# A routed-expert stage: experts of up to 64 tokens in whole fp32 products, and their place in the order

## The chip, the core and the metric

The kernel runs on one core of one Trainium2 chip. The metric is the device time of one execution in microseconds. Three runs of the kernel before took 2928.57, 2928.95 and 2931.59 us, median 2928.95.

## The reference

The program is a two-layer mixing block (gated scans, differential attention) followed by a second block, on 1024 tokens of 1024 features, in fp32. The change lies in the second block's routed experts. Each token picks 2 of 32 experts, and each expert computes

```
y = (silu(x @ w1[e]) * (x @ w3[e])) @ w2[e]      # w1, w3: 1024 x 512, w2: 512 x 1024
```

on its tokens' rows; the rows are weighted by their gates and added to the residual stream. The weights of one expert are 6 MB of fp32, those of all 192 MB.

## The kernel before, in words

Up to about 2075 us the kernel computes the first block, the convolution and recurrence of the second, and the routing. Then come 32 experts, one after the other, and after about 2805 us a final stage (a gated projection and a norm) that needs every expert's rows.

**Ranks and rooms.** The routing sorts the experts by their token count. Rank 0 is always expert 0, so that its weights can be loaded early; the others follow by falling count. `ROOM` (line 29) gives the rows that each rank gets: 256 for ranks 0 to 5, 128 for 6 to 12, 96 for 13 to 19 and 64 for 20 to 31. A 256 is handled as two blocks of 128 rows. `ORDER` (line 41) is the order in which the ranks are run: six groups, each of one 256 and then a slice of the ranks 6 to 31 in rising order. So the ranks of 64 stand in the last three groups: 3, 19, 20, 21, 22; 4, 23 to 26; 5, 27 to 31.

**Steps of an expert.** `expert_gather` fetches its token rows with an indirect DMA on POOL. `tokens` transposes them on TensorE (`rows_T`, line 1818) and splits them into a high part (ACT copy, rounded to fp32r) and a low part (DVE subtraction). `up`, `gate` and `down` are the three products. `down` scatters the rows with an indirect DMA on POOL to `ydd`. Line 1940's loop issues them so: gate of expert j, then gather, tokens and up of expert j+1, then down of expert j.

**Weights.** Each product has two tiles of 1 MB (`load`, line 1854), loaded on SP's in-order DMA queue into a ring of ten buffers (`raw`); a load waits until the tile ten places before it has been read. For a product in fp32r a tile is split into high and low parts (`split`, line 1637: ACT copy at line 1642, DVE subtraction at line 1643) into four split buffers (`ews`). After its split a raw tile is free.

**Products.** Blocks of more than 64 rows take `mm3` (line 371): three fp32r matmuls for each of the k slices (8 in up and gate, 4 for each half of the output in down). An expert of 64 takes another way in `mm`: high and low parts of the tokens stand side by side as the 128 columns of one stationary operand, and two matmuls (lines 1832 and 1833) multiply it by the weights' high and low parts. The product of the high part comes out in rows 0 to 63, that of the low part in rows 64 to 127, and `both` (line 1837) adds the halves on ACT and DVE. Its `down` doesn't split the weights: line 1912 multiplies the same 128 columns by the raw fp32 tile, which stays in the ring until TensorE has read it.

The order of instructions on each engine comes from the program's order as a scheduler rearranges it by its own estimate of when operands are ready.

Of the kernel before, what the change touches and what calls it, by code (L numbers as in the profile page):

```python
# [11 lines left out]
F32 = mybir.dt.float32  # L12
F32R = mybir.dt.float32r
# [3 lines left out]
AF = mybir.ActivationFunctionType  # L17
# [9 lines left out]
NE = 32  # L27

ROOM = [256] * 6 + [128] * 7 + [96] * 7 + [64] * 12
DBL = ROOM.count(256)  # L30
# [7 lines left out]
FAR = 36.0  # L38
NB = 2 * S // 128 + NE

ORDER = [q for d in range(DBL) for q in [d] + list(range(DBL + (NE - DBL) * d // DBL, DBL + (NE - DBL) * (d + 1) // DBL))]


def _chunks():
# [176 lines left out]
def r32(ap):  # L221
    return ap.bitcast(F32)
# [7 lines left out]
def kernel(ctx: ExitStack, tc: tile.TileContext, A: dict, out: bass.AP, upto=99, dbg=None):  # L230
    nc = tc.nc
    V, G, SC, T, SY = nc.vector, nc.gpsimd, nc.scalar, nc.tensor, nc.sync
# [138 lines left out]
    def mm3(ps, ah, al, bh, bl, first, last):  # L371
        T.matmul(ps, ah, bh, start=first, stop=False)  # L372
        T.matmul(ps, ah, bl, start=False, stop=False)  # L373
        T.matmul(ps, al, bh, start=False, stop=last)  # L374

    def feat(ps_pool, w, c0, m, half):

        wh, wl = w
        p = ps_pool.tile([128, 512], F32, tag="acc", name="pF")
        t = slice(half * 512, half * 512 + 512)  # L380
        for k in range(8):
            mm3(p[:m], wh[:, k, c0:c0 + m], wl[:, k, c0:c0 + m], ATh0[:, k, t], ATl0[:, k, t], k == 0, k == 7)
        return p

    def tokm(ps_pool, w, n, i, c0=0, at=None, tag="acc"):

        wh, wl = w
        th, tl = at or (ATh0, ATl0)
        p = ps_pool.tile([128, 512], F32, tag=tag, name="pK")
        t = slice(i * 128, i * 128 + 128)  # L390
        for k in range(8):
            mm3(p[:, :n], th[:, k, t], tl[:, k, t], wh[:, k, c0:c0 + n], wl[:, k, c0:c0 + n], k == 0, k == 7)
        return p
# [328 lines left out]
    for l in range(DEPTH):  # L722
# [104 lines left out]
        for i in range(8):  # L827
            p = tokm(pa, wi, 256, i)
# [18 lines left out]
        for half in range(2):  # L847
            t = slice(half * 512, half * 512 + 512)
            p = feat(pa, wg, 0, 32, half)
# [3 lines left out]
        for i in range(8):  # L853
            p = tokm(pa, wv, 256, i)
            SC.activation(gvv[:, i, :], p[:, :256], AF.Copy)
        with tc.high_priority(AHEAD):
            for tt in range(2):
# [4 lines left out]
                for j in range(2):  # L862
                    t = slice(j * 512, j * 512 + 512)
                    p = pm.tile([128, 512], F32, tag="mm", name="pu")
# [12 lines left out]
                    a, pU = scan_intra(sw, pm, o, False, gvv, tt * 128, j)  # L877
# [351 lines left out]
    def half(j):  # L1229
        return slice(j * 512, j * 512 + 512)  # L1230
# [25 lines left out]
    def conv_tile(f):  # L1256
        w = load_w(wp, A["w2in"][f], 8, 256, G)
        if f in PE_CONV:
            return conv_blocks(f, w)
        u = shifted("u")  # L1260
        for j in range(2):
            us = u[:, 32 + j * 512:544 + j * 512]
            SC.activation(us, feat(pa, w, 0, 128, j), AF.Copy)
            sg = bt.tile([128, 512], F32, tag="sg", name="sgc", bufs=2)
            SC.activation(sg, feat(pa, w, 128, 128, j), AF.Sigmoid)
            G.tensor_tensor(us, us, sg, op=OP.mult)

        for t in (half(0), half(1)) if f == 0 else (slice(0, S),):
            y, at = Y[f][:, t], lambda k: u[:, 2 + k + t.start:2 + k + t.stop]
            SC.activation(y, at(0), AF.Identity, scale=cw[:, f, 0:1], bias=VC("cb")[:, f:f + 1])  # L1270
            for k in range(1, 31):
                V.scalar_tensor_tensor(y, at(k), cw[:, f, k:k + 1], y, op0=OP.mult, op1=OP.add)
# [136 lines left out]
    with act_set("sigmoid_and_others", True):  # L1409
        blocks = [conv_tile(f) for f in range(4)]  # L1410
# [208 lines left out]
    ew = ews.enter_context(tc.tile_pool(name="ew", bufs=2))  # L1619
    rings.append(xw.enter_context(tc.tile_pool(name="raw2", bufs=6, side="right")))  # L1620
    ewx = xw.enter_context(tc.tile_pool(name="ewx", bufs=3, side="right"))
    first = []
# [14 lines left out]
    def split(s_, eng):  # L1637

        j = wturn[0] % 4
        wturn[0] += 1  # L1640
        w = whs[j >= 2].tile([128, 2, 4, 512], F32R, tag="w", name="ews")
        SC.activation(w[:, 0], s_, AF.Copy)  # L1642
        eng.tensor_tensor(w[:, 1], s_, r32(w[:, 0]), op=OP.subtract)  # L1643
        return w[:, 0], w[:, 1]

    with tc.tile_pool(name="rw", bufs=1) as rw, tc.tile_pool(name="rp", bufs=1, space=PSUM) as rp, \
# [129 lines left out]
        for c in range(2):  # L1776
            wh = ew.tile([128, 2, 512], F32R, tag="xh", name="wpleh", bufs=3)
            wl = ew.tile([128, 2, 512], F32R, tag="xl", name="wplel", bufs=3)
# [4 lines left out]
        for i in range(0, 8, 2):  # L1783
            eo = [ew.tile([128, D], F32, tag="ys", name="eo") for _ in range(2)]
            for c in range(2):
                for n in range(2):
                    p = pp.tile([128, 512], F32, tag="acc", name="pe")
# [30 lines left out]
    def rows_T(src, n, th, tl, m):  # L1818

        for g in range(0, m, 4):  # L1820
            p = ept.tile([128, 4, 128], F32, tag="mm", name="pT")
            for j in range(4):
                T.transpose(p[:, j, :n], src[:n, (g + j) * 128:(g + j + 1) * 128], ident[:n, :n])  # L1823
            last = (SC.activation(th[:, g:g + 4, :n], p[:, :, :n], AF.Copy),
                    V.tensor_sub(tl[:, g:g + 4, :n], p[:, :, :n], r32(th[:, g:g + 4, :n])))
        return last

    def mm(n, p, ah, al, k, bh, bl, first, last):


        if n <= 64:
            T.matmul(p, ah[:, k, :], bh, start=first, stop=False)
            T.matmul(p, ah[:, k, :], bl, start=False, stop=last)
        else:
            mm3(p[:n], ah[:, k, :n], al[:, k, :n], bh, bl, first, last)

    def both(dst, p, n):
        SC.activation(dst, p[64:64 + n], AF.Copy)
# [8 lines left out]
    class Expert:  # L1847
# [2 lines left out]

        def __init__(self, e, blocks):
            self.e, self.blocks = e, blocks

        def load(self, name):
            src = A[name][ds(self.e, 1)].rearrange("o c p k f -> c p (o k f)")
            r = []
            for c in range(2):
                s_ = raw()
                SY.dma_start(s_.rearrange("p a b -> p (a b)"), src[c])
                r.append(s_)  # L1860
            return r

        def tokens(self):
            self.X = []
            for xb, n, dst in self.blocks:
                xh = ew.tile([128, 8, 128], F32R, tag="xh", name="xh", bufs=3)
                xl = xh[:, :, 64:] if n <= 64 else ew.tile([128, 8, 128], F32R, tag="xl", name="xl", bufs=3)
                self.last = rows_T(xb, n, xh, xl, 8)
                self.X.append((xh, xl))

        def product(self, raws):
            ps = [eph.tile([128, 512], F32, tag="h", name="h") for _ in self.blocks]
            for c in range(2):
                wh, wl = raws[c] if isinstance(raws[c], tuple) else split(raws[c], V)
                for (xb, n, dst), (xh, xl), p in zip(self.blocks, self.X, ps):
                    for k in range(4):
                        mm(n, p, xh, xl, c * 4 + k, wh[:, k], wl[:, k], (c, k) == (0, 0), (c, k) == (1, 3))
            return ps

        def up(self, raws):  # L1880
# [15 lines left out]
        def down(self, raws):  # L1896
            Y2 = []
            for (xb, n, dst), hs in zip(self.blocks, self.hs):
                hh = ew.tile([128, 4, 128], F32R, tag="hh", name="hh")
                hl = hh[:, :, 64:] if n <= 64 else ew.tile([128, 4, 128], F32R, tag="hl", name="hl")  # L1900
                rows_T(hs, n, hh, hl, 4)
                Y2.append((hh, hl, ew.tile([128, D], F32, tag="ys", name="ys")))
            for c in range(2):
                whole = self.blocks[0][1] <= 64
                if not whole:
                    wh, wl = split(raws[c], V)
                for (xb, n, dst), (hh, hl, ys) in zip(self.blocks, Y2):
                    p = epy.tile([128, 512], F32, tag="y", name="py")
                    for k in range(4):
                        if whole:  # L1910

                            T.matmul(p, r32(hh[:, k, :]), raws[c][:, k], start=k == 0, stop=k == 3)
                        else:
                            mm(n, p, hh, hl, k, wh[:, k], wl[:, k], k == 0, k == 3)
                    if n <= 64:
                        both(ys[:n, half(c)], p, n)
                    else:
                        SC.activation(ys[:n, half(c)], p[:n], AF.Copy)
                    if c:
                        G.indirect_dma_start(out=ydd, out_offset=bass.IndirectOffsetOnAxis(ap=dst, axis=0),  # L1920
                                             in_=ys[:n], in_offset=None)
# [14 lines left out]

    x = ranked(ORDER[0])
    with tc.issue_after(x.last[0].ins), tc.issue_after(x.last[1].ins):
        w3 = [split(s_, V) for s_ in first[2:4]]
    for j, q in enumerate(ORDER):  # L1940
        x.gate(x.load("w3") if j else w3)
        late = x
        if j + 1 < NE:
            x = ranked(ORDER[j + 1])
        late.down(late.load("w2") if j else first[4:6])
# [169 lines left out]
```

## Time and profile before

| | |
|---|---|
| median of 3 runs | 2928.95 us |
| profiled execution | 2938.82 us, its span 2936.7 us |
| TensorE (PE) busy | 2705.7 us (92%) |
| VectorE (DVE) busy | 1832.6 us (62%) |
| ScalarE (ACT) busy | 1351.8 us (46%) |
| GpSimd (POOL) busy | 740.5 us (25%) |
| read from and written to HBM | 367.25 MB and 76.68 MB, 151 GB/s over the span |

The profile is of one execution. A window is given in us from the start of the span; for each window the profile tells how long each engine was busy, the granted clock of TensorE as a share of full speed (1.00 is 2.4 GHz), the mean busy share of the 16 DMA engines and the rate that they moved. TensorE's matmuls overlap in the records: each one's end is modelled, so the step from one to the next is shorter than the time of one, and a busy PE is not PE at its peak. An fp32 matmul is recorded as two instructions, an fp32r one as one. A few per cent of the matmul records can be missing.

### The profile page before, as it was taken

To read this page: it belongs to the slowest core of one execution; us is meant where nothing else is said; L and a number is where in the kernel's file an instruction comes from. 1 tells how busy PE (TensorE), PEld (TensorE's weight loads), DVE (VectorE), ACT (ScalarE), POOL (GpSimd) and SP (SyncE) were. 2 spreads that over 40 slices of the span, in tenths; PEclk is the share of its full clock that TensorE was granted. 3 is DMA by queue.
4 is the path that set the end of the run, shared out by engine and by line. 5 is a ranking of instruction groups with operands and counts; after the bars stand their busy time and mean duration, and the time that the engine had idled before them with its cause. 6 is when DMAs were issued, how large, how long until landed. Compare 5 with 4: busy or idle time off the path is not lost. (4 is left out here: it accounts for less than half of the span.)

```text
span 2936.7 us, 39989 instructions
## 1 busy us (share of the span) xinstructions
PE 2705.7 (92%) x15462; PEld 2156.6 (73%) x15462; DVE 1832.6 (62%) x2614; ACT 1351.8 (46%) x2126; POOL 740.5 (25%) x564
## 2 busy tenths in 40 slices
PE   7999998998999999989989999788899999899968
PEld 6887887755988878877559887687677767556558
DVE  6766564476358675644763692855677686665676
ACT  5343322465343433224653324633576675555545
POOL 1323131143214232311431434501121121211122
PEclk9999999999999999999999999899899999999989
DMA  4122223332321222233323222053898998778851
GB/s 153 62 78 67 92 81 83 94 101 83 119 89 57 80 79 76 82 83 94 101 80 119 96 90 88 29 182 135 322 364 295 348 353 296 296 277 331 336 222 73
DMA packets 140214, 446.78 MB, mean 152 GB/s; under 512 B 14432, under 2 KB 51360, under 8 KB 113760
## 3 DMA queue, kind: packets, MB, share of 16 engines
q1 hardware_dynamic: 131040, 412.26, 40.3%
q0 software_dynamic: 8960, 31.72, 3.0%
q8 instruction: 127, 2.08, 0.3%
q14 instruction: 87, 0.71, 0.1%
HBM read 367.25 MB, written 76.68 MB: 151 GB/s over the span
## 5 line engine op out<-in xcount | busy, mean ns | idle before, releaser
L1643 DVE TENSOR_TENSOR ews<-raw,ews 128x2048 fp32r<-128x2048 f32 x168 | 387.7, 2314 | 171.8 <-ACT ews L1642 170.7
L372 PE MATMUL pK<-wh,ATh 128*128 128x256 f32 x1280 | 375.0, 294 | 26.0 <-DVEq L616 10.3
L373 PE MATMUL pK<-wl,ATh 128*128 128x256 f32 x1280 | 371.9, 291 | 7.3 <-DVE wl L355 7.3
L1642 ACT ACTIVATE ews<-raw 128x2048 fp32r<-128x2048 f32 x172 | 327.2, 1912 | 106.9 <-PE h L374 73.4
L374 PE MATMUL pK<-wh,ATl 128*128 128x256 f32 x1280 | 368.0, 289 | 1.8 <-POOL ATl L1407 1.8
L372 PE MATMUL pF<-ATh,wh 128*128 128x512 f32 (+1 forms) x800 | 321.5, 403 | 0.8 <-ACT ATh L342 0.4
L373 PE MATMUL pF<-ATl,wh 128*128 128x512 f32 (+1 forms) x800 | 320.5, 401 | 0.2
L374 PE MATMUL pF<-ATh,wl 128*128 128x512 f32 (+1 forms) x800 | 319.1, 399 | 0.0
L372 PEld LDWEIGHTS pK<-wh,ATh 128*128 128x128 f32 x1280 | 250.9, 196 | 39.9 <-issue 23.4
L373 PEld LDWEIGHTS pK<-wl,ATh 128*128 128x128 f32 x1280 | 251.0, 196 | 14.3 <-DVE wl L355 8.1
L374 PEld LDWEIGHTS pK<-wh,ATl 128*128 128x128 f32 x1280 | 249.8, 196 | 5.4 <-issue 2.7
L998 DVE TENSOR_REDUCE sm<-pS 128x1 f32<-128x1024 f32 x128 | 156.2, 1221 | 112.2 <-PE pS L995 112.2
L1000 ACT ACTIVATE e<-pS,sm 128x1024 f32<-128x1024 f32 x128 | 142.4, 1112 | 171.8 <-DVE sm L998 166.0
L372 PEld LDWEIGHTS pF<-ATh,wh 128*128 128x128 f32 (+1 forms) x800 | 150.1, 188 | 39.1 <-issue 3.8
L373 PEld LDWEIGHTS pF<-ATl,wh 128*128 128x128 f32 (+1 forms) x800 | 150.1, 188 | 38.5 <-issue 5.7
L374 PEld LDWEIGHTS pF<-ATh,wl 128*128 128x128 f32 (+1 forms) x800 | 149.9, 187 | 36.7 <-issue 4.0
L373 PE MATMUL h<-ews,xh 128*128 128x512 f32 (+1 forms) x416 | 166.0, 399 | 8.8 <-DVE ews L1643 8.8
L372 PE MATMUL h<-ews,xh 128*128 128x512 f32 (+1 forms) x416 | 167.6, 405 | 5.1 <-ACT ews L1642 4.4
L374 PE MATMUL h<-ews,xl 128*128 128x512 f32 (+1 forms) x416 | 165.5, 399 | 0.0
L1843 POOL DMA_INDIRECT xb<-hfd,tab x38 | 61.4, 1615 | 402.8 <-PE pT L1823 394.1
L372 PE MATMUL pK<-wo,ATh 128*128 128x256 f32 x512 | 148.6, 290 | 10.5 <-ACT ATh L1188 10.5
L373 PE MATMUL pK<-wo,ATh 128*128 128x256 f32 x512 | 147.0, 287 | 0.0
(464 smaller groups left out, 6280.3 us busy)
## 6 DMA issues: line engine op xcount, KB each, us to landing
raw<-in_w_dram SPq DMA_DIRECT2D x192, 1024.0 KB, 8.9
ws<-in_wp_dram SPq DMA_DIRECT2D x64, 512.0 KB, 4.4
xd<-x SPq DMA_DIRECT2D x24, 512.0 KB, 2.6
x<-xd SPq DMA_DIRECT2D x17, 512.0 KB, 4.6
x<-in_x_dram SPq DMA_DIRECT2D x16, 512.0 KB, 6.6
sgd<-sgb SPq DMA_DIRECT2D x32, 256.0 KB, 2.0
sg<-sgd SPq DMA_DIRECT2D x32, 256.0 KB, 3.0
yd<-oT SPq DMA_DIRECT2D x32, 256.0 KB, 2.0
```

Source lines behind the costliest of these rows:

```text
L372: T.matmul(ps, ah, bh, start=first, stop=False)
L373: T.matmul(ps, ah, bl, start=False, stop=False)
L374: T.matmul(ps, al, bh, start=False, stop=last)
L998: put("dve", lambda: V.tensor_reduce(sm[:, c:c + 1], pf, axis=AX.X, op=OP.max, negate=True))
L1000: put("act", lambda: SC.activation(ec, pf, AF.Exp, bias=sm[:, c:c + 1], accum_out=sm[:, 2 + c:3 + c]))
L1642: SC.activation(w[:, 0], s_, AF.Copy)
L1643: eng.tensor_tensor(w[:, 1], s_, r32(w[:, 0]), op=OP.subtract)
L1843: G.indirect_dma_start(out=xb[:n], out_offset=None, in_=hfd, in_offset=bass.IndirectOffsetOnAxis(ap=idx, axis=0))
```

## The change

Experts of 64 take all three products in fp32 with unsplit weights. Their tokens are transposed into one fp32 tile of 64 columns (no split). The products for even k go to rows 0 to 63 of the PSUM tile, those for odd k to rows 64 to 127, which are two halves of the array's columns; `both` adds them as it did. Larger experts compute as before. The new order of the ranks is 0, 6, 31, 7, 30; 1, 8, 29, 9, 28; 2, 10, 27, 11, 26, 12; 3, 13, 25, 14, 24; 4, 15, 23, 16, 22; 5, 17, 21, 18, 19, 20.

```diff
-ORDER = [q for d in range(DBL) for q in [d] + list(range(DBL + (NE - DBL) * d // DBL, DBL + (NE - DBL) * (d + 1) // DBL))]
+ORDER = []
+for _d in range(DBL):
+    _few = list(range(NE - 1 - 2 * _d, NE - 3 - 2 * _d, -1))
+    _some = list(range(DBL + (NE - 12 - DBL) * _d // DBL, DBL + (NE - 12 - DBL) * (_d + 1) // DBL))
+    ORDER += [_d] + [q for p in zip(_some, _few) for q in p] + _some[2:]
+if ROOM[ORDER[-1]] > 64:
+    ORDER[-2:] = ORDER[:-3:-1]
...
-            last = (SC.activation(th[:, g:g + 4, :n], p[:, :, :n], AF.Copy),
-                    V.tensor_sub(tl[:, g:g + 4, :n], p[:, :, :n], r32(th[:, g:g + 4, :n])))
+            last = (SC.activation(th[:, g:g + 4, :n], p[:, :, :n], AF.Copy),)
+            if tl is not None:
+                last += (V.tensor_sub(tl[:, g:g + 4, :n], p[:, :, :n], r32(th[:, g:g + 4, :n])),)
...
+    def few(p, a, k, b, first, last):
+        q = k % 2 * 64
+        T.matmul(p[q:q + a.shape[2]], a[:, k, :], b, start=first, stop=last)
...
         def tokens(self):
-                xh = ew.tile([128, 8, 128], F32R, tag="xh", name="xh", bufs=3)
-                xl = xh[:, :, 64:] if n <= 64 else ew.tile([128, 8, 128], F32R, tag="xl", name="xl", bufs=3)
+                if n <= 64:
+                    xh, xl = ew.tile([128, 8, n], F32, tag="xh", name="xt", bufs=3), None
+                else:
+                    xh, xl = (ew.tile([128, 8, 128], F32R, tag=t, name=t, bufs=3) for t in ("xh", "xl"))
...
         def product(self, raws):
             for c in range(2):
+                if self.few:
+                    for k in range(4):
+                        few(ps[0], self.X[0][0], c * 4 + k, raws[c][:, k], c == 0 and k < 2, c == 1 and k >= 2)
+                    continue
...
         def down(self, raws):
-                        if whole:
-                            T.matmul(p, r32(hh[:, k, :]), raws[c][:, k], start=k == 0, stop=k == 3)
+                        if self.few:
+                            few(p, hh, k, raws[c][:, k], k < 2, k >= 2)
```

## Rows read from the trace of the kernel before

**Rows 1.** Windows, the whole expert stage: busy us (instructions) by engine, clock, DMA, rate.
```profile
core 0: us, PE busy (x) PEld busy (x) DVE busy (x) ACT busy (x) POOL busy (x), PEclk, DMA share, GB/s
2075.00:2805.00 730.00, 682.48 (x2904) 492.30 (x2904) 487.18 (x367) 437.28 (x419) 126.39 (x72) 0.97 0.85 320
```

**Rows 2.** Windows, its first and second part and the final stage.
```profile
2075.00:2430.00 355.00, 342.33 (x1581) 265.57 (x1581) 258.17 (x172) 236.08 (x209) 64.55 (x37) 0.99 0.90 347
2430.00:2805.00 375.00, 340.15 (x1324) 226.73 (x1323) 229.02 (x196) 201.21 (x211) 61.84 (x36) 0.96 0.79 295
2805.00:2937.00 132.00, 99.60 (x832) 98.90 (x832) 98.82 (x102) 70.11 (x145) 31.64 (x17) 0.89 0.43 162
```

**Rows 3.** Windows, two stretches around rank 4.
```profile
2550.00:2575.00 25.00, 25.00 (x101) 17.62 (x100) 10.33 (x9) 9.34 (x10) 2.53 (x3) 1.00 0.58 208
2575.00:2600.00 25.00, 20.67 (x87) 15.49 (x86) 13.91 (x13) 11.76 (x13) 1.80 (x2) 0.86 0.90 332
```

**Rows 4.** Waits of SP's queue, 2430 to 2805: us in total, times, longest.
```profile
SPq L1859 <- DVE ews L1643: 144.4, 29, 10.3
SPq L1859 <- PE py L1912: 89.8, 13, 21.3
```

**Rows 5.** The same, 2075 to 2430.
```profile
SPq L1859 <- DVE ews L1643: 286.1, 81, 10.8
SPq L1859 <- DMA raw<-in_w_dram: 2.0, 1, 2.0
```

**Rows 6.** Windows, PE's instructions of tile h in a 64's products.
```profile
2757.08:2762.70 5.62, 5.62 (x23) 1.00 1.01 402
```

**Rows 7.** Windows, PE's instructions of line 1912: one expert's down product.
```profile
2762.90:2770.03 7.13, 7.13 (x16) 1.00 1.02 425
```

**Rows 8.** Timeline of PE from 353.6: start, us, what, operands, count (records missing where x2).
```profile
353.76 0.44 PE L788 MATMUL pO<-A,gvv 128*64 128x128 f32 x4
354.13 0.49 PE L790 MATMUL pO<-Qi,S 128*128 128x128 f32 x2
354.55 0.43 PE L788 MATMUL pO<-A,gvv 128*64 128x128 f32 x2
354.91 0.49 PE L790 MATMUL pO<-Qi,S 128*128 128x128 f32 x2
355.33 0.44 PE L788 MATMUL pO<-A,gvv 128*64 128x128 f32 x4
...
356.90 0.33 PE L788 MATMUL pO<-A,gvv 128*64 128x128 f32 x2
```

**Rows 9.** Timeline of PE from 99.74: eight pairs of row halves.
```profile
99.74 0.37 PE L542 MATMUL pf<-Qd,Kd 64*128 64x128 f32 x1
99.75 0.37 PE L542 MATMUL pb<-Qd,Kd 64*128 64x128 f32 x1
...
100.51 0.27 PE L542 MATMUL pf<-Qd,Kd 64*128 64x128 f32 x1
100.52 0.27 PE L542 MATMUL pb<-Qd,Kd 64*128 64x128 f32 x1
100.62 0.27 PE L542 MATMUL pf<-Qd,Kd 64*128 64x128 f32 x1
100.63 0.27 PE L542 MATMUL pb<-Qd,Kd 64*128 64x128 f32 x1
```

**Rows 10.** Timeline of PE at 475.23: two pairs of row halves, 512 columns moving.
```profile
475.23 1.13 PE L995 MATMUL pS<-KH,QS 64*128 64x512 f32 x4
```

**Rows 11.** Groups of instructions, 2430 to 2805: busy us, mean ns, idle before.
```profile
L1643 DVE TENSOR_TENSOR ews<-raw,ews 128x2048 fp32r<-128x2048 f32 x72 | 164.1, 2288 | 85.3 <-ACT ews L1642 85.2
L1642 ACT ACTIVATE ews<-raw 128x2048 fp32r<-128x2048 f32 x71 | 134.7, 1909 | 46.2 <-PE h L1833 20.1 <-PE h L374 18.3 <-DMA raw<-in_w_dram 4.5
L1825 DVE TENSOR_TENSOR xh<-pT,xh 128x256 fp32r<-128x256 f32 x24 | 9.7, 412 | 0.0
L1825 DVE TENSOR_TENSOR hh<-pT,hh 128x256 fp32r<-128x256 f32 x12 | 5.0, 418 | 3.3 <-ACT hh L1824 3.3
```

More of the change, by code (lines that the diff above doesn't have):

```diff
@@ L1823, in rows_T @@
                 T.transpose(p[:, j, :n], src[:n, (g + j) * 128:(g + j + 1) * 128], ident[:n, :n])
-            last = (SC.activation(th[:, g:g + 4, :n], p[:, :, :n], AF.Copy),
-                    V.tensor_sub(tl[:, g:g + 4, :n], p[:, :, :n], r32(th[:, g:g + 4, :n])))
-        return last
[L1828 to L1835, printed above, removed]
+            last = (SC.activation(th[:, g:g + 4, :n], p[:, :, :n], AF.Copy),)
+            if tl is not None:
+                last += (V.tensor_sub(tl[:, g:g + 4, :n], p[:, :, :n], r32(th[:, g:g + 4, :n])),)
+        return last
+    def few(p, a, k, b, first, last):
+        q = k % 2 * 64
+        T.matmul(p[q:q + a.shape[2]], a[:, k, :], b, start=first, stop=last)
     def both(dst, p, n):
@@ L1852, in __init__ @@
             self.e, self.blocks = e, blocks
+            self.few = blocks[0][1] <= 64
         def load(self, name):
@@ L1876, in product @@
                     for k in range(4):
-                        mm(n, p, xh, xl, c * 4 + k, wh[:, k], wl[:, k], (c, k) == (0, 0), (c, k) == (1, 3))
+                        mm3(p[:n], xh[:, c * 4 + k, :n], xl[:, c * 4 + k, :n], wh[:, k], wl[:, k],
+                            (c, k) == (0, 0), (c, k) == (1, 3))
             return ps
@@ L1898, in down @@
             for (xb, n, dst), hs in zip(self.blocks, self.hs):
-                hh = ew.tile([128, 4, 128], F32R, tag="hh", name="hh")
-                hl = hh[:, :, 64:] if n <= 64 else ew.tile([128, 4, 128], F32R, tag="hl", name="hl")
+                if self.few:
+                    hh, hl = ew.tile([128, 4, n], F32, tag="hh", name="ht"), None
+                else:
+                    hh, hl = (ew.tile([128, 4, 128], F32R, tag=t, name=t) for t in ("hh", "hl"))
                 rows_T(hs, n, hh, hl, 4)
@@ L1903, in down @@
             for c in range(2):
-                whole = self.blocks[0][1] <= 64
-                if not whole:
+                if not self.few:
                     wh, wl = split(raws[c], V)
@@ L1909, in down @@
                     for k in range(4):
-                        if whole:
-                            T.matmul(p, r32(hh[:, k, :]), raws[c][:, k], start=k == 0, stop=k == 3)
+                        if self.few:
+                            few(p, hh, k, raws[c][:, k], k < 2, k >= 2)
                         else:
-                            mm(n, p, hh, hl, k, wh[:, k], wl[:, k], k == 0, k == 3)
+                            mm3(p[:n], hh[:, k, :n], hl[:, k, :n], wh[:, k], wl[:, k], k == 0, k == 3)
                     if n <= 64:
```

## The prediction, before the run

> **What bounds the kernel now.** I read the windows first, over the stage that the change touches (the 32 experts, 2075 to 2805 us), then SP's waits in it, then the steps of the matmuls. Over the whole stage PE is busy 682 of 730 us, the DMA engines 0.85 of it (620 us), DVE 487 and ACT 437 [rows 1]. So PE leads and DMA is close behind; neither vector engine is near. The stage is not even. In the first 355 us, where the large experts stand, PE idles 12.7 us, its clock is 0.99 and DMA stands at 0.90. In the last 375 us, where the twelve experts of 64 tokens (the few) stand nearly in a row, PE idles 34.9 us, the clock is 0.96 and DMA is at 0.79 [rows 2]: both resources have slack at the same time, so something between them fails. One place shows it: from 2550 to 2575 PE is full on a 256-token expert while DMA falls to 0.58, and in the next 25 us PE loses 4.3 us and runs at a clock of 0.86 [rows 3]. SP's waits name the cause: loads held for "PE py L1912", 89.8 us in 13 waits, the longest 21.3, a wait that the first stretch does not have [rows 4, 5]. L1912 is the down product of a few expert, which reads its two weight tiles straight from the load ring; it stands on PE behind the next expert's up product, and the ring of ten cannot turn past it.
>
> **The change part by part.** *Products of the few.* Now up and gate are 16 fp32r matmuls each (two passes for 8 k). A run of 23 takes 5.62 us, 0.244 us each [rows 6], so 32 take 7.8. The down product is 8 fp32 matmuls, which the trace records as 16 instructions: 7.13 us, 0.446 each [rows 7]. Together 14.9 us an expert. Afterwards all three are fp32: 24 products, 48 instructions, each with 64 columns, even k in one half of the array, odd k in the other. What one instruction costs hangs on whether the halves run at once. The trace of before has such work: L788 writes two 64-column halves, and its four records start and end within 0.44 us where PE's neighbours, two full instructions of the same length, take 0.49 [rows 8]. L542, split by rows instead, shows eight pairs whose partners start 0.01 us apart and which follow at 0.11 us [rows 9]; 0.11 for 128 columns is 0.446 for 512, so a pair costs what one full instruction costs. I take 24 pairs x 0.446 = 10.7 us, a gain of 4.2 us an expert, 51 over twelve. The ends: no overlap at all, 48 x 0.446 = 21.4, a loss of 6.5, 77 in all; and the row-split burst at 512 columns, two pairs in 1.13 us [rows 10], 0.565 a pair with its start and its end in it, 13.6 an expert, a gain of 1.3, 16 in all. I take the first because a burst of two pairs carries its start, a run of eight does not.
>
> The Trainium skill weighs against the full gain: "TensorE: Matmul & The Clock Gate", section "Measured speedup vs the span model", gives 2.38 times for three column tiles of 32 columns, 0.79 of ideal. At that share a pair would be 0.446 / 0.79 = 0.56 us by an estimate from that page, which is the second rival below; no run here shows column halves in a long stream of 512 columns.
>
> *Switching the array between halves and whole.* In rows 8 the two kinds alternate: five starts of L788 from 353.76 to 356.90 are four periods of 0.785 us. Each holds two pair steps and two full ones, 4 x 0.11 = 0.44; the other 0.34 is two switches, 0.17 each. A few expert's products stand on PE in some four pieces, with a large expert's products around each, so 8 switches that are not there now: 1.4 us, 16 in all (4 switches: 8; 14 switches: 29). PE's net gain is 51 - 16 = 35 us.
>
> *Splits that go.* Four tiles each are no longer split: 48 x 2.29 = 110 us of DVE, 48 x 1.91 = 92 of ACT, and 36 subtractions of 0.41 = 15 of DVE [rows 11]. Neither engine bounds the stage (487 and 437 of 730), so I count nothing for the busy time. What comes with it: the four split buffers serve the large experts alone, and the few's first product waits for one ACT copy instead of a copy, a subtraction and a split. If that cover were gone, 4.2 us of split latency per few product would show; it goes rather than comes.
>
> *Order.* The few stand one by one behind experts of 96 or 128 tokens, two in each group of a 256-token expert; the last expert is again a 64. The same 38 gathers and scatters on POOL and the same 192 loads on SP are issued, in another order; SP's in-order queue now takes a few expert's six tiles between those of large ones. PE per group: the 256 and 128 experts keep their work, so a pair of large and few asks PE for less time than its loads take, and the 256 gives it back. What evenness is worth is bounded by the late stretch's excess over the early one: idle 34.9 against 12.7 x 375 / 355 = 13.4, so 21.5 us; clock 0.96 against 0.99 over 375 us, 11 us; 33 in all [rows 2]. Nothing at the other end, or below (the third rival). DMA limits it: its 620 us are the same work, and 620 / (730 - 35 - 33) = 0.94, above the 0.90 of the early stretch. I take two thirds, 22 us; the stage is then 673 us with DMA at 0.92. What is late next is DMA, at the ends of the few.
>
> *A wait that is added.* PE itself now waits for the tiles of the few, where ACT did. Behind a few product in PE's in-order queue stand the next large expert's products, so a late tile stops those as well; ACT's and DVE's evictions wait for PE in turn. At 0.92 DMA is rarely late by more than the ring's lead, so nothing is counted beyond the third that I left off.
>
> **The sum.** 51 - 16 + 22 = 57 us. Against the profiled execution's own time, 2938.8 us (span 2936.7), that is 2882. The median of the runs is 2929.0, 0.34% lower; nothing in the stage explains that, so I take the 57 off the median: 2872.
>
> **Rivals.**
> 1. *The halves don't overlap*: the change then doubles PE's work for the few. 77 + 16 - 22 = 71 us slower, 3000. Rows 8 and 9 speak against it.
> 2. *Pairs are slower than one full instruction*: 0.565 us instead of 0.446. 16 - 16 + 22 = 22 us faster, 2907. For it: the only pairs of 512 columns are at that price [rows 10]; against it: they carry their start.
> 3. *The load ring stalls at every few expert* (the slower side). Today 24 tiles are read by PE straight from the ring and cost SP 89.8 us of waits; then it is 72 tiles, each held until PE, in order, comes to it. If DMA stays at the late stretch's 0.79 all along, the stage is 620 / 0.79 = 785 us, 55 slower: 2984. It decides at a DMA share of 0.85: below that the stage is longer than today's 730. For it: rows 3 and 4. Against it: the long wait arises behind a 256-token expert's up product, and only four few experts stand just ahead of one in the new order; behind a 128 the hold is half as long, while five pairs of tiles are ahead.
> 4. *Both run full*: the stage comes down to the DMA engines' 620 us, 110 faster, 2819. Against it: no stretch of this length holds more than 0.90.
>
> **How the numbers follow.** Chances: the forecast 0.62 (its own range 2840 to 2900), rival 1 0.05, rival 2 0.13, rival 3 0.15, rival 4 0.05. The range runs to 2835 below, since a gain beyond 94 us needs rival 4, and to 2930 above, which takes in rival 2 and the mild part of rival 3; that leaves out rival 1, most of 3 and most of 4, some 2 in 10. Within 0.2% (6 us, about what a measurement of this kernel can tell from no change) fall a piece of rival 3 and a piece of 2, 0.05; slower are rival 1 and the rest of 3, 0.17; faster is what is left, 0.78.
>
> **What would show it.** For the products: twelve experts with 48 instructions of 128x64, partners 0.01 us apart, 16 of them in about 3.6 us. For the switches: an extra 0.17 us where such a run meets a full one. For the splits: 48 fewer of L1642 and L1643. For evenness: a DMA share of about 0.92 over the whole stage, PE idle about 5%, a clock near 0.99, and SP waits for a few product with none near 20 us. Wrong would be: partners 0.446 us apart; a DMA share at or under 0.85; PE idling ahead of the few's products for raw tiles by more than some 40 us; or a stage that shrinks while the final stage after it grows by as much.

## The result and the profile after

The changed kernel takes 2890.91 us (median of 4 runs, 2885.57 to 2899.68) against 2930.27 us of the kernel before on the same chip: a ratio of 0.9864, 95% interval 0.9844 to 0.9884, 39 us faster. Forecast were 57 us. The sign and the range hold; a third of the gain is missing. The experiments show one term of the sum with the wrong sign and others that were too small, which partly make up for it.

The profiled execution took 2893.1 us, span 2891.2, which is 45.7 us less than the one before. Nearly all of it comes from the expert stage: from the first product to the end of the last it takes 682 us, 726 before (first line: before, second: after); the final stage behind it is as long as it was (132 and 133 us).

```profile
2077.30:2803.60 726.30, 680.67 (x2897) 490.72 (x2896) 486.48 (x366) 436.09 (x417) 126.39 (x72) 0.98 0.85 321
```

```profile
2076.50:2758.80 682.30, 648.87 (x2898) 426.48 (x2896) 367.29 (x282) 346.20 (x370) 106.71 (x72) 0.96 0.88 339
```

The windows of the kernel after, first the whole stage, then its two parts and the final stage (columns as in rows 1):

```profile
2075.00:2765.00 690.00, 650.37 (x2904) 427.79 (x2903) 370.25 (x284) 351.62 (x374) 107.60 (x73) 0.96 0.87 337
...
2075.00:2430.00 355.00, 337.61 (x1506) 230.98 (x1506) 191.80 (x146) 181.36 (x191) 55.28 (x38) 0.96 0.88 340
2430.00:2765.00 335.00, 312.77 (x1400) 196.81 (x1398) 178.46 (x139) 170.26 (x184) 52.32 (x35) 0.96 0.86 332
2765.00:2891.00 126.00, 99.23 (x832) 98.53 (x832) 95.09 (x102) 65.94 (x143) 30.74 (x16) 0.89 0.44 168
```

Against [rows 1, 2]: PE is busy 32 us less, and DVE and ACT lost 117 and 86 us. The stage is even now, but even in the wrong way. The first part had 12.7 us of PE idle and a clock of 0.99; now it has 17.4 and 0.96. The second part fell from 34.9 to 22.2 us of idle, and its clock stayed at 0.96. DMA stands at 0.87, not at the 0.92 of the forecast.

The products cost what the sum says. PE's timeline of the kernel after, around one down product of a few expert (columns as in rows 8):

```profile
2193.28 0.39 PE L381 MATMUL h<-ews,xl 128*128 128x512 f32 x1
2193.60 3.65 PE L1840 MATMUL py<-raw,ht 128*64 128x512 f32 x16
2197.18 0.50 PE L379 MATMUL h<-ews,xh 128*128 128x512 f32 x1
2197.52 0.39 PE L380 MATMUL h<-ews,xh 128*128 128x512 f32 x1
```

Sixteen instructions take 3.65 us, where [rows 7] has 7.13 for the same count in whole-array form: two halves for the price of one. The switches can be read off too. From 2193.28 to 2197.52 there are two whole steps (0.235 each, the step from 2193.04 to 2193.28) and eight pair steps of 0.43: 3.91 us. The row shows 4.24, so two switches cost 0.33, 0.17 each, as worked out from [rows 8]. Their number is another matter. An unbroken run of few products (no whole-width product inside it, transposes not counted) has one switch at each end, and PE's timeline of the stage shows about 33 such runs, so some 66 switches, 11 us, where the sum has 96 and 16 us.

PE now waits for other things. PE's waits of the kernel before in its last 375 us, and of the kernel after in the whole stage (total us, times, longest):

```profile
PE h L1832 <- DVE xh L1825: 12.0, 3, 4.1
PE py L1912 <- DVE hh L1825: 8.6, 4, 4.3
PE h L1833 <- DVE ews L1643: 5.2, 5, 3.6
PE h L1832 <- ACT ews L1642: 2.3, 2, 1.8
```

```profile
PE pT L1830 <- DVE hs L1907: 11.0, 4, 2.9
...
PE h L379 <- ACT xh L1831: 5.1, 5, 1.6
PE h L379 <- ACT ews L1649: 4.2, 3, 1.6
PE h L381 <- DVE xl L1833: 3.4, 2, 1.7
PE h L380 <- DVE ews L1650: 2.8, 3, 1.8
```

Before, 28 us of idle in the late part belonged to the few experts' own products, which waited for the low parts and splits that the change does away with. After, those lines are gone. In their place the large experts' products (L379 to L381) wait for their tokens' copies and splits, and transposes wait for a gate's last multiplication (`hs`). (The line left out, 10.4 us for `xb`, is the wait for the stage's first token rows, 6.8 us before.) All four waits of the `hs` line stand before a few expert's transposes (64 rows), three of them behind the next large expert's up product, as here:

```profile
2249.84 0.46 PE L1830 MATMUL pT<-ident,hs 64*128 64x64 f32 x4 [2.84 <-DVE hs L1907]
```

The longest of SP's waits for a few product fell from 21.3 us [rows 4] to 14.7, so that sign of the prediction holds, but their total rose from 89.8 us to 180.5 (102.0 and 78.5), with three times as many tiles read by PE:

```profile
SPq L1865 <- DVE ews L1650: 309.0, 59, 17.0
SPq L1865 <- PE h L1840: 102.0, 25, 14.7
SPq L1865 <- PE py L1840: 78.5, 20, 13.4
```

### The profile page after: what moved, and what is told of

It reads as the page before. It is cut to its first block, busy times and chain, and to the rows that moved or that the text cites. A ratio compares the mean times of both kernels' runs of the same rounds, so it can differ in the third digit from the quotient of the medians.

```text
span 2891.2 us, 39821 instructions
## 1 busy us (share of the span) xinstructions
PE 2669.6 (92%) x15462; PEld 2087.7 (72%) x15462; DVE 1712.3 (59%) x2530; ACT 1262.3 (44%) x2078; POOL 722.4 (25%) x564
## 5 line engine op out<-in xcount | busy, mean ns | idle before, releaser
L379 PE MATMUL pK<-wh,ATh 128*128 128x256 f32 x1280 | 373.8, 293 | 24.3 <-DVEq L623 10.7
L1650 DVE TENSOR_TENSOR ews<-raw,ews 128x2048 fp32r<-128x2048 f32 x120 | 277.3, 2325 | 187.6 <-ACT ews L1649 185.8
L381 PE MATMUL pK<-wh,ATl 128*128 128x256 f32 x1280 | 366.7, 288 | 1.8 <-POOL ATl L1414 1.8
L379 PE MATMUL pF<-ATh,wh 128*128 128x512 f32 (+1 forms) x800 | 321.4, 403 | 1.7 <-ACT g L1335 0.9
L381 PE MATMUL pF<-ATh,wl 128*128 128x512 f32 (+1 forms) x800 | 319.5, 400 | 0.1
L1649 ACT ACTIVATE ews<-raw 128x2048 fp32r<-128x2048 f32 x124 | 234.6, 1910 | 156.5 <-PE h L381 62.6
L379 PEld LDWEIGHTS pK<-wh,ATh 128*128 128x128 f32 x1280 | 249.2, 195 | 38.8 <-issue 16.1
L381 PEld LDWEIGHTS pK<-wh,ATl 128*128 128x128 f32 x1280 | 247.9, 194 | 5.5 <-issue 2.8
L379 PEld LDWEIGHTS pF<-ATh,wh 128*128 128x128 f32 (+1 forms) x800 | 150.1, 188 | 40.3 <-issue 4.0
L379 PE MATMUL h<-ews,xh 128*128 128x512 f32 (+1 forms) x416 | 168.6, 410 | 9.3 <-ACT xh L1831 5.1
L381 PEld LDWEIGHTS pF<-ATh,wl 128*128 128x128 f32 (+1 forms) x800 | 149.9, 187 | 36.9 <-issue 4.3
L381 PE MATMUL h<-ews,xl 128*128 128x512 f32 (+1 forms) x416 | 168.0, 405 | 3.4 <-DVE xl L1833 3.4
L1848 POOL DMA_INDIRECT xb<-hfd,tab x38 | 53.2, 1399 | 456.1 <-PE pT L1830 447.6
L379 PE MATMUL pK<-wo,ATh 128*128 128x256 f32 x512 | 149.0, 291 | 9.7 <-ACT ATh L1195 9.7
```

Source lines behind the costliest of these rows:

```text
L1848: G.indirect_dma_start(out=xb[:n], out_offset=None, in_=hfd, in_offset=bass.IndirectOffsetOnAxis(ap=idx, axis=0))
```

## Experiments

**The two halves of the change, each alone.** The theory was that the products carry the gain; the rival, that the order lets them pay. The first kernel is the change with the old `ORDER`, the second the kernel before with the new one.

> The new products, with the order of the ranks as it was. If the gain comes from the products alone (a pair of halves for the price of one instruction, PE the bound wherever they stand), the time is 2880 to 2895 us. If the few in a row are bound by their loads (six tiles of 2.49 us, 15 us an expert, against 12 us of PE), the shorter products wait for tiles: DMA share over 0.95 in the last 250 us, PE idle or at a low clock there, and 2905 to 2930 us; the order would then be what lets the products pay.

Measured: 2868.97 us, ratio 0.9769 (0.9727 to 0.9811), below both expectations: faster than the whole change.

> The new order with the products as they were. If evenness is worth what was forecast (22 to 33 us from the last 375 us), 2895 to 2908 us. If the order by itself is worth nothing, since each stall that goes at the few comes back at the large experts, 2922 to 2938 us.

Measured: 2952.26 us, ratio 1.0069 (1.0046 to 1.0091), outside both expectations: the order by itself makes the kernel slower. The stage in the window from first to last product, the products alone (first fence) and the order alone (second):

```profile
2077.00:2736.00 659.00, 628.33 (x2897) 416.83 (x2896) 368.30 (x282) 349.16 (x369) 104.69 (x72) 0.99 0.90 349
```

```profile
2073.14:2816.04 742.90, 691.76 (x2897) 493.55 (x2896) 485.03 (x366) 435.82 (x417) 115.49 (x72) 0.96 0.83 314
```

With the products alone the stage takes 659 us, the clock is 0.99 and DMA 0.90, all without touching the order. The few's runs on PE are about 12, so some 24 switches, 4 us, and not 16. Against the kernel before, PE is busy 52 us less and idle 15 us less (31 us against 46). With the order alone DMA falls to 0.83 and PE's worst wait is the few's own chain, 28.5 us where it was 8.6 before:

```profile
PE py L1918 <- DVE hh L1831: 28.5, 8, 5.5
```

So the products are worth 62 us (2930.8 to 2869.0), the order costs 21 us with the old products (2930.8 to 2952.3) and 22 us with the new (2869.0 to 2890.9; by the ratios to their own runs of before, 0.9769 and 0.9864, it is 28). In both kernels with the new order PE's largest wait behind the first product stands between a few expert's own gate and down: `hh` above, `hs` in the change.

**Whether the halves run at once.**

```diff
-        q = k % 2 * 64
-        T.matmul(p[q:q + a.shape[2]], a[:, k, :], b, start=first, stop=last)
+        m = a.shape[1] // 2
+        q = k // m * 64
+        T.matmul(p[q:q + a.shape[2]], a[:, k, :], b, start=k % m == 0, stop=k % m == m - 1)
```

> As after the change, but the first half of the k slices goes to one half of the array's columns and the second half to the other, in turn, instead of alternating. Same instructions, same operands, same sums. If the price of a pair rests on neighbours that stand in different halves, a product takes 6.9 us instead of 3.65, 3.3 x 36 = 119 us of PE more, and the time is 2970 to 3010 us. If 64 columns are cheap whatever stands beside them, or if an instruction for the other half is started early across several, the time stays within 15 us of after, 2891.

Measured: 2944.04 us, ratio 1.0047 (1.0026 to 1.0068): 53 us slower than the change, 13 slower than before. Products of few experts in PE's timeline say why it is neither 15 nor 100, first a down product, then an up or gate, then a stretch of up and gate products:

```profile
2153.32 3.70 PE L1841 MATMUL py<-raw,ht 128*64 128x512 f32 x16
...
2163.31 7.08 PE L1841 MATMUL h<-raw,xt 128*64 128x512 f32 x16 [0.22 <-ACT xt L1831]
```

```profile
2132.71 7.19 PE L1841 MATMUL h<-raw,xt 128*64 128x512 f32 x24
```

In a down product four instructions for one half are followed by four for the other; they still run side by side (3.70 us). In this up or gate product eight are followed by eight, and they run in turn: (7.08 - 0.59) / 15 = 0.43 us a step, with no neighbour. In the third line 24 instructions take (7.19 - 0.59) / 0.43 + 1 = 16 steps, so eight of them had a neighbour. The gain does rest on the other half's work being near in the program: partners four instructions apart (the down products) always ran side by side, partners eight apart ran in turn in one product and partly side by side elsewhere. What decides there stays open. The trace doesn't tell which half an instruction works on, the scheduler may have moved some, and in an up or gate product of this kernel the second half also reads the second weight tile, which a down product's second half doesn't.

> The new products in the old order, but every k slice goes to rows 0 to 63: 48 instructions an expert in one half of the array, none beside another (the two halves' sum is replaced by two halved copies of the one). PE's steps alone say 48 x 0.43 = 20.6 us against 14.9 before, 69 us slower than before: 2990 to 3005 us. If the few's splits and low parts held PE as well, their going gives part of that back: the idle time for them in the kernel before is 28 us and the half clock behind it some 10 to 15, so 2950 to 2970 us.

```diff
-        T.matmul(p[q:q + a.shape[2]], a[:, k, :], b, start=first, stop=last)
+        T.matmul(p[:a.shape[2]], a[:, k, :], b, start=k == 0, stop=k == a.shape[1] - 1)
```

Measured: 2978.23 us, ratio 1.0146 (1.0114 to 1.0177), 47 us slower than before, between the two expectations. The steps alone cost 69 us more by the expectation; that sum sets 0.43 us a step against an old price worked out with 0.446, and with 0.446 for both it is the 77 of rival 1. So 22 to 30 us come back, with PE's work on the few made longer. The stage shows 22 of them as idle time of PE that is gone, 24 us in this window against 46 before:

```profile
2077.40:2847.20 769.80, 746.23 (x2897) 453.82 (x2896) 369.37 (x282) 348.43 (x369) 103.56 (x72) 0.99 0.81 302
```

This bears out that the splits and low parts held PE up, measured without the pairs. It isn't their exact worth, since PE's longer work also covers more of everyone's waits.

**Why the new order costs.** Three theories were tried on the order as changed: tokens too late, splits ahead of short evictions in ACT's and DVE's queues, too little work on PE to cover a large expert's chain.

> As after the change, but the gather and the transposes of the next expert are issued ahead of the gate product of the current one. After the change PE stands idle in 9 places, 11 us, with the next expert's transposes done and their copies not, and its clock falls behind some of them. If the transposes are simply issued too late, these places go and the time is 2868 to 2882 us. If what holds the copies is the splits ahead of them in ACT's and DVE's in-order queues, the wait moves elsewhere and the time is 2885 to 2900 us.

Measured: 2893.6 us, ratio 0.9869 (0.9829 to 0.9909). The waits for `xh` go from PE's list, and "PE py L379 <- ACT ys L1931: 15.0, 7, 5.0" and a split wait of 12.2 us stand in their place. The time is the same.

> The change as it is, with each split of a large expert that follows a few expert queued on ACT and DVE behind that few expert's evictions of the same step. After the change ACT waits 57.9 us in 17 places for a split buffer that PE's py matmuls still read (3.3 us in 5 before), with a few expert's evictions behind it. If this head-of-line wait is what the new order costs, the time comes near that of the products with the old order: 2866 to 2880 us, and those waits fall under 20 us. If the order costs by something else (the large experts' tokens, the load ring), 2885 to 2900 us; if the splits then come too late, over 2900.

```diff
+            with tc.issue_after(ends[0].ins), tc.issue_after(ends[1].ins):
+                return split(s_, V)
```

Measured: 2900.5 us, ratio 0.9881 (0.985 to 0.9912), no better than the change. The wait that it aims at nearly went, from the first line below (after) to the second (this kernel), so the head-of-line wait is not what the order costs:

```profile
ACT ews L1649 <- PE py L381: 57.9, 17, 9.1
```

```profile
PE py L381 <- DVE hl L1833: 10.8, 11, 1.4
PE h L379 <- ACT xh L1831: 9.3, 4, 3.9
PE py L379 <- ACT hh L1831: 8.9, 10, 2.4
...
ACT ews L1649 <- PE py L381: 5.0, 1, 5.0
```

What took its place is telling: 21 times PE now stands before a large expert's down product, waiting for that expert's own high or low part (`hh`, `hl`).

> The change as it is, but the down product of a 96 or 128 that has a few expert behind it is issued after that expert's gate instead of before it: two few products (7.3 us) instead of one (3.65) stand on PE between a large expert's gate and its down. If the order costs because one few product is too short a cover for a large expert's eviction, transposes, copy and subtraction, the waits of the large experts' transposes and products for them shrink and the time falls to 2868 to 2880 us. If not, 2885 to 2900 us.

```diff
             x = ranked(ORDER[j + 1])
+            if x.few and not late.few and len(late.blocks) == 1:
+                x.gate(x.load("w3"))
+                gated = True
         late.down(late.load("w2") if j else first[4:6])
```

Measured: 2868.56 us, ratio 0.9777 (0.9754 to 0.9799), its interval below that of the change: 22 us come back, the whole cost of the order. The stage in its window:

```profile
2075.00:2742.00 667.00, 638.37 (x2896) 419.58 (x2894) 366.11 (x280) 345.76 (x369) 99.54 (x72) 0.98 0.89 348
```

DMA is back at 0.89 and the clock at 0.98, with the few in the same places. Between a large expert's gate and its down stand now two few products of 3.65 us instead of one. Where a 96 or 128 follows, it is that expert's up, a product of 24 steps, 5.6 us. A few's up was short before the change too, 16 x 0.244 = 3.9 us, but it followed a large expert three times in the old order and does so twelve times in the new one. The chain that this work must cover is a multiplication on DVE, four transposes, a copy on ACT and a subtraction on DVE, with a split of 1.9 or 2.3 us ahead of it in either queue now and then.

PE's waits in this kernel don't show that it was the large experts' chain, though:

```profile
PE h L379 <- ACT xh L1831: 4.0, 5, 1.7
PE pT L1830 <- DVE hs L1907: 3.7, 2, 1.9
PE py L379 <- ACT hh L1831: 3.6, 4, 1.4
```

The large experts' waits for `xh` and `hh` were 5.1 us and none by that name in the change; what fell is the wait for `hs`, from 11.0 us, and that one stood before the few's own transposes. So the trace points at the few's chain rather than the large experts'. The edit moves a few's gate ahead of the large expert's down, so the few's chain from gate to down also gets that down as cover; and it moves two of the few's loads ahead of the large expert's. These three were not taken apart.

Nor was the order's price mostly idle time. From the first to the last product PE idles 33 us in the change, 31 with the products alone and 29 here; it is busy 649, 628 and 638 us with the same matmuls, at a granted clock of 0.96, 0.99 and 0.98. Added up over windows of 10 us, what the clock lacks to full speed is 24, 8 and 12 us, upper bounds, since PE's idle time is in them. So the clock is the larger part of what the order costs and of what the later down gives back. Of the rest, the change's some 42 switches more than in the old order are about 7 us; the later down kept nearly all of those (31 runs).

**How the cost goes with the order.** Steps from a few to a larger expert, counted in each order (the expectations say 12 for the change; the last few has no successor, so it is 11).

> The new products with a third order: two few experts together right behind each 256, then the 96s and 128s (in the last group the two few last). The steps from a few to a larger expert are 5, against 12 after the change and 2 in the old order. If each such step costs about 2.3 us (23 us over ten steps), the time lies 7 us above the old order, 2873 to 2880 us. If DMA near its limit in the old order's last 216 us (0.96) is what holds that one, spreading the pairs gains: 2845 to 2862 us. If any few expert away from the end costs as it did, 2885 or more.

> The new products, few experts one by one as after the change, but a few ahead of each 96 or 128 instead of behind it, so that no 256 follows a few. Single steps from a few to a larger expert stay at 11. If every such step costs, the time stays at 2883 to 2897 us. If what costs is a 256 that follows a few (its two blocks of tokens wait there, four places after the change), it falls to 2866 to 2878 us.

> The new products with the few in four runs of three, each right behind a 256 (ranks 2 to 5): 3 steps from a few to a larger expert, 2 in the old order, 5 in pairs, 12 after the change. If the steps alone set the cost, 2868 to 2878 us. If the old order's last 216 us, with DMA at 0.96, also hold it, the earlier start of the few gains some: 2850 to 2866 us.

> The new products with all twelve few at the end: no step from a few to a larger expert. If such steps are all that an order can cost, 2858 to 2868 us. If the few in a row are bound by their loads (15 us and a gather and scatter against 12 us of PE), DMA stands at 1.0 over the last 190 us, PE idles there, and the time is 2885 to 2910 us.

| kernel, new products | steps | us | ratio to before, interval |
|---|---|---|---|
| few last (e11) | 0 | 2881.47 | 0.9823 (0.9801 to 0.9845) |
| old order (e1) | 2 | 2868.97 | 0.9769 (0.9727 to 0.9811) |
| in threes behind a 256 (e10) | 3 | 2873.97 | 0.981 (0.978 to 0.9841) |
| in pairs behind a 256 (e6) | 5 | 2879.26 | 0.9811 (0.9782 to 0.9841) |
| the change | 11 | 2890.91 | 0.9864 (0.9844 to 0.9884) |
| one by one, no 256 behind a few (e8) | 11 | 2901.94 | 0.9897 (0.9865 to 0.9928) |

From 2 steps up the time rises with the steps, by 2.4 to 5 us a step counted from the old order, though neighbours in the table overlap. The steps themselves are not the price: the change with the later down has the same 11 and is as fast as the old order. That no 256 follows a few (e8) doesn't help; the time is above both of its expectations. At no step at all (e11, between its two expectations) another bound shows: the twelve few in a row want 72 tiles faster than they come. The last 178 us of that kernel, and PE's longest wait in its stage:

```profile
2570.00:2748.00 178.00, 140.65 (x640) 45.66 (x636) 36.89 (x56) 43.36 (x87) 16.29 (x18) 0.92 1.02 403
```

```profile
PE h L1834 <- DMA raw<-in_w_dram: 25.8, 13, 5.2
```

DMA is full and PE idles 37 us. In the old order, with runs of three to five few, that wait is 2.1 us, and its steps are two.

**An attempt to beat both.**

> A version meant to beat both: the new products, two few together in the middle of each group between 96s or 128s (5 steps from a few to a larger expert), and the down product of the large expert ahead of them issued after the first few's gate. If the short cover at each step is what an order costs, and the later down removes most of it, half the steps leave 2850 to 2866 us. If the later down already removed all that can be removed, and the rest is DMA or the products themselves, 2866 to 2880 us.

Measured: 2883.6 us, ratio 0.9841 (0.9818 to 0.9863): a miss, above both expectations. Fewer steps and the later down together are slower than either the old order or the later down alone. PE idles 36 us of 675 there, on many waits of which none is over 8.1 us in total. Why the two don't add stays open.

## Why the prediction was right in sign and a third of its gain is missing

- *The products.* Right, and to its price: 16 instructions in 3.65 us (forecast about 3.6), 10.9 us an expert against 10.7. A step of a pair is 0.43 us, so rival 1 is out, and so is rival 2 with its 0.565 us. The Trainium skill ("TensorE: Matmul & The Clock Gate", "Measured speedup vs the span model") gives 2.38 times for three tiles of 32 columns, 0.79 of ideal; three such tiles side by side were not read in any run here. Two tiles of 64 columns reach the full factor of two within a run of eight pairs, and 1.8 with the run's two switches (16 x 0.43 = 6.9 us against 3.44 + 0.33).
- *The switches.* Right in price, 0.17 us each, as in the row that it was taken from; too many were counted. For 16 us in the sum the runs show about 4 with the old order and 11 in the change.
- *The splits that go.* Mis-sized. Their busy time off the bound was rightly counted as nothing. But the prediction says of their latency only that it "goes rather than comes" and puts 0 in the sum. The products alone gave 62 us where 51 - 16 = 35 were counted: 27 us more, of which 12 are switches that were not there. PE's idle time, where the splits' latency shows, fell by 15 us: 28 us of waits for the few's low parts and splits went, others came. These waits could have been read before: they stand in PE's waits of the late stretch, which the prediction did not open.
- *The order.* This is the step that failed: "I take two thirds, 22 us". It took the late stretch's excess of idle and half clock for a fault of the few standing in a row. That stretch's idle was mostly the few's own chain, 28 of 35 us, which the products cure in place (the old order with new products has a clock of 0.99 and DMA at 0.90). The new order cost 21 or 22 us instead, a swing of 43 or 44. Products alone less the order is 62 - 22 = 40, and 39 were measured; that only adds up measured parts and is no test of the terms. That the total still came within the range is in part luck: a gain of 22 that was a loss of 22 met 27 us that were not counted.
- *Rival 3* had the right sign for the order, but its ring that stalls at every few expert is not what the runs show. DMA did stay below the forecast (0.87), yet with the later down the same order of experts and the same ring reach 0.89 and 2868.6 us, with more waiting of SP for few products, not less (139.9 and 80.9 us against 102.0 and 78.5).
- *The wait that is added*, PE standing for tiles of the few, was rightly small in the change: it is not among PE's waits. It decides only where the few stand last.

What is shown: the products' gain, the price of a pair and of a switch, the order's cost with either products, and that issuing a few's gate ahead of the large expert's down takes this cost back. What is argued: how the gain divides between shorter products and waits that are gone, and that the cover's length, 3.65 us against a chain with a split in it, is the mechanism of the order's cost. The waits that fell are not the large experts', and the last kernel, which should have gained by it, didn't.

## What to carry to other kernels

Before short steps are moved between the long ones of a loop that is ordered by hand, ask what work on the bound engine stands between each expert's gate and its down, and what chain on the vector engines it covers. Here such a move cost 21 or 22 us with the old products as with the new, and another place for one product took it back. Idle time of a stretch belongs to a wait by name before it belongs to an order; open the bound engine's own waits of that stretch, and not only its busy share and the DMA queue's. A price per switch needs a count from the order of the instructions, too. Two matmuls with 64 columns each, in opposite halves of the array and near each other in the program, cost as one; here alternating halves and halves that changed after four instructions did so every time.

## What the runs showed of the hardware

Work for the array's two halves ran side by side when the program has the partner four instructions further on (16 in 3.70 us) and not, in the product shown, at eight (7.08 us); 24 instructions elsewhere in that run did so in part (7.19 us). A change between 128 columns and 64 cost 0.17 us (0.33 for the two around a run of eight pairs). A clock that falls is part of the price of short stalls: in the kernel after, from 2247 to 2272 us, PE idles 4.1 us, 2.8 of it behind a large expert's products, and the granted clock of those 25 us is 0.86, partly at the lower level of 1.2 GHz; waits of at most 1.6 us behind the first product of the kernel before left its first part at 0.99.

```profile
2247.00:2272.00 25.00, 20.92 (x82) 11.91 (x81) 12.33 (x8) 12.24 (x14) 5.34 (x4) 0.86 0.58 210
```
